# Hybrid backbone block: S5 and recurrent inputs of segment 2 are projected ahead of values, keys and queries

## The chip, the cores and the metric

The kernel runs on one core of one Trainium2 chip. The metric is the device time of one execution in microseconds (us), from the first to the last instruction of the program. Engines are named TensorE (PE in the profile; PEld is its weight load), VectorE (DVE), ScalarE (ACT), GpSimd (POOL) and SyncE (SP), which here only issues DMAs.

## The reference

One layer of a backbone block over 2048 latent tokens and 256 context tokens, 1024 features. Cut to what matters here:

```python
z = modulated_rmsnorm(x) @ w_in          # one combined input projection
q, k, v, gate, lr, lx, lgate, u = split(z)
gla = gated_linear_attention(q, k, v, lr)     # two directions, chunks, states
lru = rglru(short_conv(lx))                   # two directions, linear scan
s5  = s5(u)                                   # two directions, scanned in column-major grid order
cat = concat(norm(gla) * silu(gate), lru * gelu(lgate), glu(gelu(s5 + D * u)))
x   = x + gate1 * (cat @ w_out)
x   = x + gate2 * (square(relu(modulated_rmsnorm(x) @ w1)) @ w2)
out = rmsnorm(x)
```

The latent scans start from the final states of the context, in both directions. The S5 scan goes over the grid by columns, so each of its runs needs the input u of all four segments of latent tokens.

## The kernel before

Tokens are worked in segments: the context (`c`, 256) and four latent segments 0 to 3 of 512. All products of the projections are done in three matmuls on exact high and low parts (`mm3`, L324 to L326: `wH*hH`, `wH*hL`, `wL*hH`). A projection tile is 128 output features of one segment: eight steps over the features, 24 matmuls of 512 columns, into an `acc` tile of PSUM; ScalarE copies it out (`evac`, L331) and GpSimd's queue writes it to DRAM scratch (`put`). Its weights are loaded by the SP queue and split by `wsplit` (L318 load, L319 ScalarE cast, L320 VectorE difference) into a few rotating buffers. The values (`v_cols`) go the other way round, 272 columns at a time, and end in small transposes (L387, L390).

The tiles of a segment have three groups: `A4` (`su0 su1`, the S5 input; `lx0 lx1`, the input of the recurrent unit), `B6` (values, keys, queries) and `G4` (the gates). `in_proj` walks a list of (names, segments) that is written out by hand; `("h", s)` normalizes and splits the input of a segment (`h_of`, `hprep`, L287 to L307), for which two pairs of buffers rotate.

Beside this main stream run side streams, each a Python generator that yields the time that its step is reckoned to take, or the name of an event that has to be emitted first. `Streams.run` lets the side stream that is furthest behind take a step whenever its reckoned time, its yields times a ratio, has fallen behind the main stream's. A projection tile counts 5.2 units, a block of values 2.8. The side streams:

- `xstream` (ratio 3.0): S5 matrices (`s5_prep`) and tables (`s5_tables`), then 16 S5 runs (`s5_run`), each 1.8 units times 3.0. A run waits for its half of the S5 input in all segments (`su0` or `su1`). It loads about 1 MB, multiplies (L783), turns and scans on VectorE (L790 to L815), multiplies again (L820 to L824) and stores its result (L829).
- `ystream`, `ystream2` (ratio 0.8): the GLA's first part (`gla_prep`, L873 to L953) by pairs of blocks: segment 2 first, then 3, in each of the two streams. A segment's part waits for its `v0 v1 k0 k1 q0 q1`. Four working buffers (`wg`) hold one pair, so a stream's segment 3 follows when segment 2 has given them up. `gla_ends` (L965) comes last and gives the event `gla`.
- the recurrent unit (`lru`, ratio 4.0): forward over the context, 0, 1, backward over 3, then forward over 2 and 3; it waits for `lx0`, `lx1`.
- `read_out(3)` (ratio 0.7): it waits for `gla` and for the gates of segment 3. Blocks 3 and 2, then 1 and 0: loads (L1064 to L1067), scores (L1078, L1079), masks (L1081 to L1083), the backward state (L1028), products (L1091, L1092), a norm (L1099 to L1110) and the split of the result (L1015, L1016). The same four `wg` buffers hold one pair of blocks. Then the gate of the recurrent unit and, after the event `s5`, that of the S5 group (L1146).

`out_proj(3)` follows `in_proj` in the main stream: first products with six of the eight input parts, then the first phase's memory is given up (`open_ff`), then the rest, and the second norm. The second phase is the MLP of segments 3, 2, 1, 0, with the read-out of the next segment as a side stream.

The order in which instructions are emitted sets their priority; a scheduler then writes each engine's own queue, in which an instruction that is ready by its reckoning can come ahead of an earlier one that is not. Some parts (`wsplit`, `put`, `hprep`) are given a higher priority. On the chip each engine runs its queue in order.

Of the kernel before, what the change touches and what calls it, by code (L numbers as in the profile page):

```python
# [8 lines left out]
F32 = mybir.dt.float32  # L9
# [7 lines left out]
P = 128  # L17
# [6 lines left out]
NS = 16          # S5 groups  # L24
T8 = 8           # tokens that share a column of the S5 input layout
T16 = 16         # S5 chunk
NCH = SEQ // T16  # latent chunks
CCH = CTX // T16  # context chunks
NP = T16 + 2     # powers of the transition
XSZ = 1312  # L30
PKW = 1408       # S5 matrices of a group: read-out 2 x 256, input 4 x 128, kernel 3 x 128
# [11 lines left out]
# columns of the packed per-feature vector table  # L43
# [9 lines left out]
# W_in column tiles of 128 features  # L53
COLS = ["su0", "su1", "lx0", "lx1", "k0", "k1", "q0", "q1", "gg0", "gg1", "gg2", "gg3", "lg0", "lg1"]
WIDX = {n: i for i, n in enumerate(COLS)}
VN = 272         # half of v and the decay ranks of one direction


class Streams:
    """Emits a main and several side streams of instructions in step.  # L60

    A stream yields the time that its step takes, or the name of an event that has to be emitted first."""
# [10 lines left out]
    def step(self, limit):  # L73
        """One step of the side stream that is furthest behind; False if none is ready before `limit`."""
        ready = [x for x in self.live if (x[3] is None or x[3] in self.done) and (limit is None or x[2] <= limit)]
        if not ready:
            return False
        x = min(ready, key=lambda y: y[2])
        x[3] = None
        try:  # L80
            r = next(x[0])
        except StopIteration:
            self.live.remove(x)
            return True
        if isinstance(r, str):
            x[3] = r
        else:
            x[2] += r * x[1]
        return True

    def run(self, main):
        """`main` with the side streams."""
        while True:
            r = next(main, None)
            if r is None:
                return
            if isinstance(r, str):
                while r not in self.done:
                    assert self.step(None), (r, [x[3] for x in self.live])
                continue  # L100
            self.tm += r
            while self.step(self.tm):
                pass
            for x in self.live:
                if x[3] is not None and x[3] not in self.done:
                    x[2] = max(x[2], self.tm)
# [12 lines left out]
def hybrid_block(ctx: ExitStack, tc: tile.TileContext, xT, ctxT, cc, cct, wmodA, wmodT, pv, win, wva, wvb, upw, lrini, lruw, s5v, gluw,  # L119
# [27 lines left out]
    # ---------------------------------------------------------------- constants  # L147
# [14 lines left out]
    gsc1 = consts.tile([P, 16], F32, name="gsc1")      # norm1*(1+sc1): latent, context  # L162
    gsc2 = consts.tile([P, 8], F32, name="gsc2")

    # DRAM scratch, one tile per token segment
# [22 lines left out]
    qq_d = dram.tile([8, P, 1024], F32, name="qq_d")      # by pairs of blocks  # L188
    kk_d = dram.tile([8, P, 1024], F32, name="kk_d")
    ds_d = dram.tile([NB, 64, 512], F32, name="ds_d")      # backward block updates  # L190
    sf_d = dram.tile([16, 64, 512], F32, name="sf_d")      # forward states that enter the blocks
    bs_d = dram.tile([64, 512], F32, name="bs_d")          # backward state carried to the next segment
    # constant rows and borders of the scratch
# [7 lines left out]
    # ---------------------------------------------------------------- pools of the first phase  # L201
# [4 lines left out]
    def slots(tag, size, bufs):  # L206
        """A rotating workspace of `bufs` slots of `size` floats a partition."""
        def w(*shape, rows=P, dtype=F32):
            n = 1
            for d_ in shape:  # L210
                n *= d_
            t = side.tile([P, size], dtype, name=tag, tag=tag, bufs=bufs)[0:rows, 0:n]
            if len(shape) == 2:
                t = t.rearrange("p (a b) -> p a b", b=shape[1])
            elif len(shape) == 3:
                t = t.rearrange("p (a b c) -> p a b c", b=shape[1], c=shape[2])
            elif len(shape) == 4:
                t = t.rearrange("p (a b c d) -> p a b c d", b=shape[1], c=shape[2], d=shape[3])
            return t
        return w  # L220
# [6 lines left out]
    def big_pair():  # L227
        """The two parts of a split operand of 512 tokens."""
# [4 lines left out]
    # ---------------------------------------------------------------- adaLN vectors  # L233
# [3 lines left out]
    # silu(c) on every partition, for the products that run along the free axis  # L237
# [8 lines left out]
    def mod_first():  # L246
        """shift and scale of the first norm, latent and context"""
# [35 lines left out]
    # ---------------------------------------------------------------- normalized, modulated, split input  # L283
    def hprep(pool, src, t0, n, hH, hL, gsc, sh):
        """Normalize and modulate n tokens of src and split them exactly into two fp32r parts."""
        x = pool.tile([P, KT, n], F32, name="x", tag="x", bufs=XB)
        S.dma_start(x, src[:, t0:t0 + n].rearrange("(k p) t -> p k t", p=P))  # L287
        # 1/rms over the features on every partition
# [20 lines left out]
    def wsplit(pool, src, shape, tag, bufs, parts=None):  # L309
        """Load a weight tile and split it exactly into two fp32r parts (in `parts`, if they are there already);  # L310
        bufs: of the load, of each part."""
# [16 lines left out]
    # ---------------------------------------------------------------- input projection  # L328
# [40 lines left out]
    def v_cols(c, chunks):  # L369
        """Half of the values, token by token, with the decay ranks of one direction."""  # L370
# [50 lines left out]
    # ---------------------------------------------------------------- RG-LRU  # L421
# [21 lines left out]
    def lru(d, order, wl=wl):  # L443
        for s in order:
# [31 lines left out]
            # gates; sigmoid(z) = (1 + tanh(z/2))/2  # L476
# [35 lines left out]
    # ---------------------------------------------------------------- S5  # L512
# [4 lines left out]
    def s5_params():  # L517
# [73 lines left out]
        def cmul(or_, oi, ar, ai, br, bi, t, conj_b=False, neg_i=False):  # L591
            """(or, oi) = a*b (conj(b) if conj_b); oi negated if neg_i."""
# [51 lines left out]
        # step[k] = e^{+-i theta T 2^k}: + on the forward half, - on the backward half  # L644
# [7 lines left out]
        # input matrix  # L652
# [20 lines left out]
        # powers by slot: E: forward j, backward 17-j;  F: forward 15-s, backward s  # L673
# [13 lines left out]
    def s5_prep(b):  # L687
# [5 lines left out]
        # C lambda^k by slot  # L693
# [22 lines left out]
        # intra-chunk kernel, both directions  # L716
# [11 lines left out]
        # shifted windows of it make the Toeplitz blocks  # L728
# [9 lines left out]
    def s5_tables(g0):  # L738
        """Phase tables of four groups by doubling."""
# [23 lines left out]
    def s5_run(g):  # L763
# [32 lines left out]
        # real scans; results shifted by one chunk so that a chunk's column holds the state that enters it  # L796
# [9 lines left out]
        # the state that enters latent chunk c sits at column c + CCH + 1 on both halves  # L806
# [25 lines left out]
    # ---------------------------------------------------------------- GLA, first part: decays and block states  # L832
# [18 lines left out]
    def gla_prep(s, blocks, other=False):  # L851
        """Decays, decayed queries and keys, block updates, forward states of pairs of blocks of a segment.

        other: in the memory that the input's norm has left."""
# [15 lines left out]
        for b in blocks:  # L870
# [19 lines left out]
            # -log_sigmoid(z) = max(-z, 0) + log(1 + exp(-|z|))  # L890
# [49 lines left out]
            # forward states  # L940
# [16 lines left out]
    def gla_ends():  # L957
        """-log_sigmoid of the (shifted) token past the end of each sequence"""
# [15 lines left out]
    # ================================================================ read-out and MLP  # L974
# [15 lines left out]
    def ws(s, n, tag="t"):  # L990
        """Workspaces of the read-out, n tiles of 512; the last segment's come before the MLP's memory is there."""
# [11 lines left out]
    def decays():  # L1003
        # exponents of the decay between a block's anchor and the state that enters it
        # forward: -c_mid/16; backward: -(c_127 - c_mid + c_0 of the next block)/16
# [14 lines left out]
    def back_step(ss, blk):  # L1020
        """backward state that enters latent block blk -> ss[64:128]"""
# [17 lines left out]
    def open_ff():  # L1039
        """The first phase's workspaces make room for the MLP's."""  # L1040
# [8 lines left out]
    def read_out(s):  # L1049
        """Read-out of the three groups of a segment."""  # L1050
# [6 lines left out]
        # GLA read-out, pairs of blocks from the last to the first as the backward state runs  # L1057
# [55 lines left out]
        # RG-LRU gate  # L1113
# [14 lines left out]
        # S5 gate  # L1128
# [24 lines left out]
    def out_proj(s):  # L1153
        """Output projection, residual and second norm of a segment."""
        early = []
        if s == 3:
            # the first products run while the S5 group's read-out comes to its end
# [33 lines left out]
        # second norm; its split result takes the place of the split read-out  # L1191
# [102 lines left out]
    # ================================================================ first phase  # L1294
# [23 lines left out]
    def ystream2():  # L1318
        for x in (2, 3):
# [13 lines left out]
                          (B6, [0, 1]), (G4, [0]), ("h", 3), (G4, [1]), ("h", 2), (A4, [3]), (B6, [3, 2]), (A4, [2]),  # L1333
# [3 lines left out]
    # ================================================================ second phase  # L1337
# [8 lines left out]
def pack(i):  # L1346
    """Lay the inputs out for the kernel; no arithmetic."""
# [38 lines left out]
    # decay projection: rank rows of the two directions and, on row 16, the bias  # L1386
# [27 lines left out]
    # constants of the shapes: identity, 1+identity, strict upper mask, block starts  # L1414
# [3 lines left out]
    low = np.tri(P, P, -1, dtype=f4)     # [j, i]: 1 where j > i  # L1418
# [25 lines left out]
```

## Time and profile before

| what | value |
|---|---|
| timed runs | 2481.51, 2481.51, 2481.74 us; median 2481.51 |
| profiled execution | span 2482.1 us; no other time is given for it |
| TensorE busy | 2347.2 us (95%), 10992 matmul records |
| VectorE busy | 1610.0 us (65%) |
| ScalarE busy | 1169.2 us (47%) |
| DMA | 364.03 MB, mean 147 GB/s |

The span is the metric as the profiled execution has it. Busy time of TensorE counts matmuls that overlap as one stretch. All times in rows of the trace are in us from the start of the span.

### The profile page before, as it was taken

How to read it: one execution, taken by the hardware profiler on the slowest of the kernel's cores; microseconds unless marked ns; L12 is line 12 of the kernel's file. 1: busy time of each engine (PE TensorE's matmuls, PEld its weight loads, DVE VectorE, ACT ScalarE, POOL GpSimd, SP SyncE). 2: the span in 40 equal slices, each digit the busy share in tenths (PEclk: the TensorE clock that was granted, in tenths of full speed). 3: DMA queues.
4: the chain of work that ended last, by engine and by line, in shares of the span. 5: the costliest groups of instructions: out<-in, count | busy, mean ns of one | idle time of the engine just before them, and what ended most of it. 6: DMA issues, size and time to landing. Idle time of an engine off the chain costs nothing.

```text
span 2482.1 us, 29891 instructions
## 1 busy us (share of the span) xinstructions
PE 2347.2 (95%) x10992; PEld 1886.0 (76%) x10992; DVE 1610.0 (65%) x2698; ACT 1169.2 (47%) x1704; POOL 100.7 (4%) x141
## 2 busy tenths in 40 slices
PE   7779999898887899999999999999999999999997
PEld 3668777877675677888877788887778888888886
DVE  6886878726786766565576656557655655655555
ACT  3764567436555645343355534336543433433333
POOL 1020111002100000000000000000000000000000
PEclk9989999999998999999999999999999999999999
DMA  7666777557775643322355322336522232333221
GB/s 258 209 201 208 223 238 227 168 174 207 253 240 181 206 135 120 101 94 93 100 177 162 118 86 93 102 102 202 159 85 94 94 102 87 126 102 102 94 94 51
DMA packets 189107, 364.03 MB, mean 147 GB/s; under 512 B 35200, under 2 KB 104144, under 8 KB 187920
## 3 DMA queue, kind: packets, MB, share of 16 engines
q1 hardware_dynamic: 183872, 346.20, 44.1%
q0 software_dynamic: 5088, 15.93, 1.9%
q8 instruction: 86, 1.41, 0.2%
q14 instruction: 61, 0.50, 0.1%
HBM read 299.76 MB, written 62.75 MB: 146 GB/s over the span
## 4 chain that ended last, share of the span: by engine, by line
PE 64%; ACT 5%; DVE 5%; DMA 3%; issue 2%; SPq 1%; POOL 0%; DVEq 0%; ACTq 0%; POOLq 0%
PE acc L324 10%; PE acc L326 9%; PE acc L325 9%; PE sa L324 9%; PE sa L325 9%; PE sa L326 9%; PE sb L324 2%; PE sb L326 2%; PE sb L325 2%; DVE wL L320 1%; ACT wH L319 1%; PE sb L1146 1%; DMA t<-lru 1%; DMA t<-kk_d 0%; DMA wR<-in_wout_dram 0%
## 5 line engine op out<-in xcount | busy, mean ns | idle before, releaser
L319 ACT CAST wH<-wR 128x1024 fp32r<-128x1024 f32 (+1 forms) x353 | 370.9, 1051 | 903.9 <-PE sa L325 432.8
L324 PE MATMUL acc<-hH,wH 128*128 128x512 f32 (+1 forms) x1576 | 629.6, 400 | 24.8 <-ACT hH L303 9.2
L320 DVE TENSOR_TENSOR wL<-wR,wH 128x1024 fp32r<-128x1024 f32 (+1 forms) x353 | 427.3, 1222 | 346.5 <-ACT wH L319 342.0
L326 PE MATMUL acc<-hH,wL 128*128 128x512 f32 (+1 forms) x1576 | 620.1, 394 | 3.2 <-DVE wL L320 3.1
L325 PE MATMUL acc<-hL,wH 128*128 128x512 f32 (+1 forms) x1576 | 617.7, 392 | 1.2 <-DVE hL L307 0.8
L1257 DVE SCALAR_TENSOR_TENSOR xa<-sa,modl,xa 128x512 f32<-128x512 f32 (+1 forms) x520 | 383.1, 741 | 197.5 <-PE sa L326 194.8
L324 PE MATMUL sa<-sH,wH 128*128 128x512 f32 (+1 forms) x1040 | 403.9, 389 | 4.6 <-DVE xa L1257 4.2
L326 PE MATMUL sa<-sH,wL 128*128 128x512 f32 (+1 forms) x1040 | 402.2, 387 | 0.0
L325 PE MATMUL sa<-sL,wH 128*128 128x512 f32 (+1 forms) x1040 | 401.9, 386 | 0.0
L324 PEld LDWEIGHTS acc<-hH,wH 128*128 128x128 f32 x1576 | 299.8, 191 | 95.3 <-ACT hH L303 10.3
L325 PEld LDWEIGHTS acc<-hL,wH 128*128 128x128 f32 x1576 | 300.1, 191 | 70.8 <-issue 6.2
L326 PEld LDWEIGHTS acc<-hH,wL 128*128 128x128 f32 x1576 | 299.5, 190 | 70.8 <-DVE wL L320 5.2
L324 PEld LDWEIGHTS sa<-sH,wH 128*128 128x128 f32 x1040 | 195.2, 188 | 49.2 <-DVE xa L1257 9.3
L326 PEld LDWEIGHTS sa<-sH,wL 128*128 128x128 f32 x1040 | 195.3, 188 | 40.8
L325 PEld LDWEIGHTS sa<-sL,wH 128*128 128x128 f32 x1040 | 195.4, 188 | 40.6 <-DVE sL L1233 0.8
L1233 DVE TENSOR_TENSOR sL<-sr,sH 128x512 fp32r<-128x512 f32 x128 | 88.2, 690 | 27.6 <-ACT sH L1232 27.5
L325 PE MATMUL acc<-wL,hH 128*128 128x272 f32 x288 | 87.8, 305 | 8.8 <-DVE wL L320 8.7
L324 PE MATMUL acc<-wH,hH 128*128 128x272 f32 x288 | 89.2, 310 | 2.0 <-ACT ev L331 1.9
L331 ACT COPY ev<-acc 128x512 f32<-128x512 f32 (+2 forms) x96 | 47.5, 495 | 85.1 <-issue 41.0
L326 PE MATMUL acc<-wH,hL 128*128 128x272 f32 x288 | 86.5, 301 | 0.0
L1232 ACT CAST sH<-sr 128x512 fp32r<-128x512 f32 x128 | 78.8, 617 | 10.8 <-PE sa L326 9.0
L1231 ACT ACTIVATE sr<-sr 128x512 f32<-128x512 f32 x128 | 80.8, 632 | 3.4
(402 smaller groups left out, 2717.2 us busy)
## 6 DMA issues: line engine op xcount, KB each, us to landing
wR<-in_w_dram SPq DMA_DIRECT2D x256, 512.0 KB
wR<-in_win_dram SPq DMA_DIRECT2D x54, 512.0 KB
wm<-in_wmodT_dram SPq DMA_DIRECT2D x32, 512.0 KB
wR<-in_wout_dram SPq DMA_DIRECT2D x32, 512.0 KB
wm<-in_wmodA_dram SPq DMA_DIRECT2D x8, 1024.0 KB
x<-in_xT_dram SPq DMA_DIRECT2D x8, 1024.0 KB
w<-pk_d SPq DMA_DIRECT2D x16, 512.0 KB
xa<-in_xT_dram SPq DMA_DIRECT2D x32, 256.0 KB
```

Of the source, the lines that this page charges most:

```text
L319: A.copy(Hf, raw)
L320: V.tensor_tensor(Lf, raw, f32(Hf), OP.subtract)
L324: T.matmul(acc, wH, hH, start=first, stop=False)
L325: T.matmul(acc, wH, hL, start=False, stop=False)
L326: T.matmul(acc, wL, hH, start=False, stop=last)
L331: A.copy(e, acc)
L1146: T.matmul(ps, gw[:, k, ct * P:(ct + 1) * P], sg[k], start=k == 0, stop=k == 1)
L1231: A.activation(r, r, AF.Square)
L1232: A.copy(sH, r)
L1233: V.tensor_tensor(sL, r, f32(sH), OP.subtract)
L1257: V.scalar_tensor_tensor(xa[:, m, a0:a1], acc, modl[:, 40 + m:41 + m], xa[:, m, a0:a1], OP.mult, OP.add)
```

## The change

In the list that `in_proj` walks, the entry of `A4` for segment 2 moves from behind `B6` of segments 3 and 2 to ahead of it. All else in the diff is comments, docstrings and blank lines.

```diff
     A4, G4, B6 = "su0 su1 lx0 lx1", "gg0 gg1 gg2 gg3 lg0 lg1", "v0 v1 k0 k1 q0 q1"
     st.run(chain(in_proj([("h", "c"), ("h", 0), (A4 + " v0 v1 k0 k1", ["c"]), ("h", 1), (A4, [0]), (A4, [1]),
-                          (B6, [0, 1]), (G4, [0]), ("h", 3), (G4, [1]), ("h", 2), (A4, [3]), (B6, [3, 2]), (A4, [2]),
+                          (B6, [0, 1]), (G4, [0]), ("h", 3), (G4, [1]), ("h", 2), (A4, [3]), (A4, [2]), (B6, [3, 2]),
                           (G4, [3]), (G4, [2])]),
                  out_proj(3)))
```

## Rows read from the trace of the kernel before

**Rows 1.** First line of the page.

```profile
span 2482.1 us, 29891 instructions
```

**Rows 2.** Stretches: length; busy us (records) of PE, PEld, DVE, ACT, POOL; clock; DMA.

```profile
422.00:500.00 78.00, 70.54 (x493) 63.95 (x492) 57.82 (x132) 38.17 (x66) 5.82 (x8) 0.93 0.56 166
500.00:545.00 45.00, 43.21 (x191) 35.33 (x189) 13.19 (x29) 8.45 (x14) 3.79 (x7) 1.00 0.60 181
545.00:666.00 121.00, 107.08 (x528) 86.41 (x527) 77.40 (x136) 72.51 (x112) 22.80 (x32) 0.96 0.71 216
666.00:771.00 105.00, 85.80 (x515) 70.87 (x514) 90.91 (x212) 69.13 (x126) 5.13 (x9) 0.94 0.73 225
...
851.00:2482.00 1631.00, 1607.49 (x7206) 1305.05 (x7205) 995.79 (x1311) 689.19 (x937) 3.71 (x6) 1.00 0.35 112
```

**Rows 3.** The same stretches, records of L783 (first matmuls of S5 runs) alone.

```profile
545.00:666.00 121.00, 7.96 (x40) 6.87 (x40) 0.96 0.71 216
666.00:771.00 105.00, 16.51 (x88) 15.27 (x88) 0.94 0.73 225
```

**Rows 4.** The same stretches, records of L324 (first of each mm3) alone.

```profile
545.00:666.00 121.00, 38.05 (x93) 17.91 (x93) 0.96 0.71 216
666.00:771.00 105.00, 14.14 (x35) 6.58 (x35) 0.94 0.73 225
```

**Rows 5.** Timeline of TensorE around an S5 run: start, length, line.

```profile
701.47 0.49 PE L823 MATMUL sa<-w 128*128 128x128 f32 x2
...
702.91 1.29 PE L783 MATMUL sa<-w 128*128 128x160 f32 x8
...
704.49 0.38 PE L1092 MATMUL mm<-wg,fs 128*128 128x128 f32 x2
```

**Rows 6.** Timeline of TensorE: GLA's first matmuls, S5's, GLA's last, read-out's first.

```profile
545.17 1.13 PE L895 MATMUL sb<-glt,upt 48*128 48x256 f32 x4
...
569.89 0.90 PE L783 MATMUL sa<-w 128*128 128x160 f32 x2 [5.41 <-ACT w L777]
...
657.77 1.05 PE L965 MATMUL sb<-wg,upt 48*128 48x2 f32 x8
...
676.72 0.37 PE L1078 MATMUL sb<-wg 64*128 64x128 f32 x1 [0.34 <-DMA wg<-kk_d]
```

**Rows 7.** Timeline of the SP queue: first load of each pair of blocks.

```profile
666.00 0.37 SPq L1064 DMA_DIRECT2D wg<-gg  x1
...
716.25 0.38 SPq L1064 DMA_DIRECT2D wg<-gg  x1
```

**Rows 8.** Timeline of VectorE: last split of the GLA read-out.

```profile
772.16 0.68 DVE L1016 TENSOR_TENSOR hL<-wg,hH 128x512 fp32r<-128x512 f32 x1
```

**Rows 9.** Groups by line, 666 to 771: count, busy us, mean ns, idle before.

```profile
L1101 ACT ACT_TABLE_LOAD x4 | 5.1, 1283 | 0.1
...
L480 PE MATMUL sb<-wl,lwt 128*128 128x512 f32 x10 | 5.1, 613 | 0.3 <-DVE wg L1081 0.3
...
L1028 DVE SCALAR_TENSOR_TENSOR fs<-fs,bdec 64x128 f32<-64x128 f32 x12 | 3.8, 349 | 2.2 <-DMA fs<-ds_d 2.0
...
L1082 DVE COPY_PREDICATED wg<-mup,sb 128x512 f32<-128x512 int32 x4 | 2.9, 722 | 0.0
```

**Rows 10.** Waits of TensorE, 545 to 771: total us, times, longest.

```profile
PE sa L823 <- DVE w L814: 18.2, 12, 5.2
...
PE sb L928 <- issue: 5.3, 1, 5.3
```

**Rows 11.** Timeline of TensorE: first matmul of the values of segment 3.

```profile
422.14 0.28 PE L324 MATMUL acc<-wH,hH 128*128 128x272 f32 x1
```

**Rows 12.** Timeline of VectorE: last low parts of segment 2's input.

```profile
421.78 1.67 DVE L307 SCALAR_TENSOR_TENSOR hL<-x,modl,hH 128x256 fp32r<-128x256 f32 x4
```

**Rows 13.** Waits of ScalarE, 545 to 771: total us, times, longest.

```profile
ACT wH L319 <- PE acc L325: 30.7, 10, 7.9
```

**Rows 14.** Ten us around the wait of L928, columns as in rows 2.

```profile
620.00:630.00 10.00, 4.71 (x17) 3.84 (x16) 7.12 (x8) 6.80 (x12) 5.10 (x6) 0.72 0.66 230
```

## The prediction

> **What bounds the kernel now.** I read the page first for the span [rows 1], then cut the span into stretches at the places where the work changes [rows 2], then counted what runs in each, then asked who waits. From 851 us to the end TensorE is busy 1607.49 of 1631 us: the MLP is bound by TensorE and nothing before it changes what it has to do, so the question is when it can begin. Before that, three stretches differ. From 500 to 545 us (keys and queries of segments 3 and 2) TensorE is busy 43.21 of 45 us and VectorE 13.19: TensorE-bound, VectorE empty. From 545 to 666 TensorE is busy 107 of 121 us. From 666 to 771 it is TensorE 85.80 and VectorE 90.91 of 105 us.
>
> What fills the last two is seen by counting. An S5 run has 8 records of L783 and a projection tile of 512 tokens 8 of L324. So 545 to 666 holds 40/8 = 5 S5 runs and 93/8 = 11.6 projection tiles; 666 to 771 holds 11 runs and 4.4 tiles [rows 3, 4]. The 16 tiles are those of segment 2's first group (4) and of the two gate groups (12). By adding the planner's yields only 4.5 of them come before the end of the GLA part; the trace has 11.6 there, so projections are pulled ahead wherever a chain makes TensorE wait, and the last 105 us are left with little filler. There the S5 runs follow each other every 105/11 = 9.5 us, since TensorE's queue has a run's first matmuls (L783) behind the last ones (L823, L824) of the run before [rows 5], and between a run's first and last VectorE has to turn and scan.
>
> The second chain is the GLA. Its first decay matmul (L895) starts at 545.17 us, the moment that q1 of segment 2 is done; its end (L965) comes at 657.77, the read-out's loads start at 666.00, its first scores at 676.72, its second pair of blocks is loaded from 716.25, and the last split of its result (L1016) starts at 772.16 [rows 6 to 8]. So from q1_2 to the first output products are 121 + 105 = 226 us. Both chains end together, around 775 us.
>
> **The change part by part.** No instruction is added or removed: four tiles (su0, su1, lx0, lx1 of segment 2) move from behind the values, keys and queries to ahead of them. The planner's sums then shift: su0_2 is done 86.4 units earlier (248.2 for 334.6), so S5 runs begin at 300.2 (the tables are ready then) and not at 334.6; the RG-LRU of segments 2 and 3 comes at 286 to 361, not 350 to 413; and q1_2, with it the whole GLA of segments 2 and 3, leaves the planner 20.8 units later (350.2 for 329.4). At 350.2 S5 runs 0 to 8 have been emitted; before, none had at 329.4. I take the new stretches in turn.
>
> *Up to q1_2, now 422 to 545.* TensorE gets more to do ahead of q1_2: four tiles of 24 matmuls at 43.21/191 = 0.226 us, the pace of 500 to 545 [rows 2], are 21.7 us; nine S5 runs at 3.02 us, the unbroken run from 701.47 to 704.49, are 27.2; two RG-LRU gate sets of 8 records at 0.51 us (5.1/10) [rows 9] are 8.2. The waits of L823, 18.2 us over 12 [rows 10], are 1.5 each on a loaded VectorE; on a free one I take 0.4, 3.6 for nine. Sum 61 us. From below: 422 to 500 holds 78 - 70.54 = 7.5 us without TensorE [rows 2], into which S5 matmuls can go: 54. From above 66: those waits doubled, and the 1.4 us of the next sentences. I take 61, since those 7.5 us are waits of TensorE's own in-order queue. The moved tiles need segment 2's normalized input at once: the values start at 422.14 and the last four parts of hL are written from 421.78 for 1.67 us [rows 11, 12]. The tiles take their k-th part only after k times 0.7 us, so nothing, at most 1.4 us; the cover is thin, and if it goes the whole queue shifts by as much.
>
> *GLA, now 545 to 666.* It finds the same company: five runs (9 to 13) and 11.6 of the 12 gate tiles, pulled ahead as before. What goes is the wait of run 0 for its own projection, 5.41 us at 569.89 [rows 6], and the slow clock behind it, 1.6 us. The other wait, L928 for 5.3 us [rows 10], stays, being GLA's own chain. So 121 - 7 = 114 us. From below: ScalarE waits 30.7 us in this and the next stretch for TensorE to release a weight buffer [rows 13], ten waits, with GLA's activations behind them in its queue; without two of the longest, 2 x 7 us, it would be 100. From above 121. I take 114.
>
> *Read-out of segment 3, now 666 to 771.* Here the S5 runs are gone but two (14 and 15), and so are both RG-LRU gate sets. A pair of blocks alone: loads 676.72 - 666.00 = 10.7 us [rows 6, 7]; three mask operations for each block at 0.72, 4.3; eight steps of the backward state at 0.35, 2.8; two table loads at 1.28 and four activations at about 0.7, 5.4; eight gains as long as those steps, 0.35, and two products of 0.7, 4.2 [rows 9]; about 68 TensorE records at 0.11 us (28 records in the 3.02 us of [rows 5]), 7; copies, squares, casts and differences not covered, 2.6. Sum 37 us, some 4 of which the two blocks overlap: 33. Two pairs, the second loaded only when the first gives up its buffers: 66 us. From above the 105 of now; between ends so far apart it lies near the first, because most of what shared VectorE's 90.91 us has left; two runs' worth on top, 68 us. As 0.4 tiles are left to fill TensorE, it stands idle here, and after waits it drops to the lower of its two levels: 0.72 granted from 620 to 630 [rows 14]. Its 7 us a pair doubled are 14 more, so 82 is the upper end; 58 the lower, if the pairs overlap more.
>
> The Trainium skill (TensorE: Matmul & The Clock Gate, section on HAM oscillation) says that idle stretches bring the throttled level back each time; the trace agrees at 620 to 630, and the rule speaks against this change. By it alone the sum would be 14 us more.
>
> *Behind it.* From 771 to 851 the output products, the reopening of the pools and the second norm follow as now, without run 15's last part: 1.5 us less, 0 to 2. The MLP's 1631 us stay.
>
> Sum: +61 - 7 - 37 - 1.5 = +15.5 us. The profiled execution took 2482.1 us, 0.6 us above the median of the runs (2481.51); so 2482.1 + 15.5 - 0.6 = **2497 us**, slower. What replaces the S5 chain as the last to end is the read-out behind a GLA that starts 61 us later.
>
> **The rivals.** *Faster: the S5 chain was the bound and its cover is free.* For it: 16 S5 runs pace the time from 569.89 to 771, VectorE is 87% busy at the end and 29% busy at 500 to 545, where nine runs move to. It decides if GLA and read-out together need less than 226 - 61 = 165 us. At the lower ends, 54 - 21 (100 for GLA) - 47 (58 for the read-out) - 2 is -16: 2466 us. Against it: 114 + 68 = 182. The Trainium skill (Perfetto Trace Analysis, Optimization Strategy) advises to interleave regimes with different most-contended engines, which is this; the trace has the two regimes, but the rule does not say what is put off. By it the time would be that of this rival.
>
> *No change: the two shifts cancel.* The queues don't follow the planner strictly (11.6 tiles for 4.5), so GLA at 104 us and the read-out at 62 would give +61 - 17 - 43 - 1.5, within a microsecond of zero: 2481 us. For it: both chains end together now. Against it: a coincidence of two sizes.
>
> *Much slower: the read-out also meets the lower clock.* The upper ends of the first and third term: +66 - 7 - 23 = +36 us: 2518. For it: the missing filler. Against it: most of the read-out is on ScalarE, VectorE and the queues.
>
> **How the numbers follow.** Forecast 0.50, faster 0.26, no change 0.13, much slower 0.11. The forecast's own range, from the mixed bounds of its terms, is 2487 to 2512. A measurement of this kernel tells some 0.2%, 5 us, from no change: faster 0.26, same 0.13, slower 0.61. The range reaches to the faster rival's 2466 and to 2520, just past the last one; each side leaves about 0.1.
>
> **What would show it.** Right: L783 first appears some 50 us ahead of 569.89 while keys and queries run; L895 of segments 2 and 3 starts near 606 us instead of 545; S5 is done before the read-out's second pair; TensorE has holes between about 725 and 790 us with waits of L1078, L1091 or the output products on loads, VectorE or ScalarE; the last L1016 of the GLA part is near 788; the stretch behind it is as long as now. Wrong in the terms: L895 before 595 (S5 found holes), GLA under 105 us (its waits were TensorE's pace, not its own), a read-out under 60 us. Wrong altogether: no hole in TensorE up to the output products.

## The result, and the profile after

The change makes the kernel slower: 2499.0 us median of four runs (2494.3 to 2501.3) against 2481.6 (2481.5 to 2481.9), a ratio of 1.0069 with a 95% interval of 1.0056 to 1.0082. The forecast was 2497. The profiled execution after has a span of 2499.5 us, 17.4 us more than [rows 1].

Stretches of the kernel after, cut where the work changes, with the columns of [rows 2]:

```profile
545.00:611.00 66.00, 60.75 (x323) 49.16 (x322) 40.04 (x96) 25.19 (x55) 3.24 (x6) 1.00 0.62 188
611.00:725.00 114.00, 97.09 (x485) 79.03 (x485) 77.30 (x135) 64.83 (x100) 18.03 (x32) 0.94 0.71 213
725.00:787.00 62.00, 40.58 (x246) 33.14 (x244) 37.16 (x90) 36.95 (x58) 1.62 (x3) 0.85 0.59 170
867.00:2499.00 1632.00, 1607.39 (x7207) 1305.30 (x7206) 995.71 (x1311) 688.20 (x937) 3.69 (x6) 1.00 0.34 112
```

The second and third answer to the GLA part and the read-out of [rows 2]. The read-out is short now, but TensorE is busy in only 40.58 of its 62 us, and its granted clock has dropped to 0.85. The MLP is the same to a tenth of a microsecond of TensorE work.

The same for L783 alone, the first matmuls of S5 runs (eight records each), as in [rows 3]:

```profile
500.00:545.00 45.00, 4.26 (x24) 3.47 (x24) 1.00 0.68 201
545.00:611.00 66.00, 7.93 (x48) 7.12 (x48) 1.00 0.62 188
611.00:726.00 115.00, 7.65 (x40) 6.42 (x40) 0.94 0.71 211
726.00:787.00 61.00, 2.59 (x16) 2.31 (x16) 0.84 0.60 172
```

Nine runs stand ahead of the GLA, five beside it, two beside the read-out, as forecast. Timelines of TensorE, the SP queue and VectorE, three engines in order; they answer to [rows 6 to 8]:

```profile
610.95 1.99 PE L895 MATMUL sb<-glt,upt 48*128 48x256 f32 x8
...
642.06 0.90 PE L783 MATMUL sa<-w 128*128 128x160 f32 x2 [7.37 <-ACT w L777]
...
725.67 1.05 PE L965 MATMUL sb<-wg,upt 48*128 48x2 f32 x8
...
787.27 0.80 PE L324 MATMUL acc<-hH,wH 128*128 128x512 f32 x1 [7.84 <-ACT hH L1015]
...
725.23 0.45 SPq L1064 DMA_DIRECT2D wg<-gg  x1
...
787.25 0.69 DVE L1016 TENSOR_TENSOR hL<-wg,hH 128x512 fp32r<-128x512 f32 x1 [0.74 <-ACT hH L1015]
```

So the GLA starts 65.8 us later than before, its ends 67.9 later, the read-out's loads 59.2 later, and the last split of the GLA's result 15.1 later. Behind that nothing is regained. Some waits of TensorE from 600 to 870 us (total, times, longest):

```profile
PE acc L324 <- ACT hH L1015: 9.2, 2, 7.8
...
PE acc L324 <- ACT hH L1201: 6.3, 1, 6.3
PE sa L823 <- DVE w L814: 6.1, 4, 4.0
...
PE sb L1078 <- DMA wg<-kk_d: 4.2, 1, 4.2
...
PE mm L1091 <- issue: 2.5, 1, 2.5
PE sb L1099 <- ACT wg L1094: 2.4, 2, 1.2
```

These are the forecast's holes: TensorE now waits for the read-out itself (the 6.3 us before L1201, in the second norm, are there before the change too). The 7.8 us are the first output products waiting for the split of the last pair. From 422 us to the MLP, TensorE is busy 372.0 of 429 us before and 376.2 of 445 after: no work was added (1976 and 1980 records), but there are 11.8 us more of idle time, and the same matmuls are busy 4.2 us longer.

### The profile page after: what moved, and what is told of

Same layout as the page of the kernel before. It is cut to its first block, busy times and chain, and to the rows that moved or that the text cites. A ratio compares the mean times of both kernels' runs of the same rounds, so it can differ in the third digit from the quotient of the medians.

```text
span 2499.5 us, 29912 instructions
## 1 busy us (share of the span) xinstructions
PE 2348.0 (94%) x10992; PEld 1882.8 (75%) x10992; DVE 1614.5 (65%) x2698; ACT 1168.7 (47%) x1704; POOL 95.9 (4%) x141
## 4 chain that ended last, share of the span: by engine, by line
PE 68%; DVE 7%; ACT 6%; DMA 4%; issue 3%; SPq 1%; POOL 0%; DVEq 0%; ACTq 0%; POOLq 0%
PE acc L324 11%; PE acc L326 10%; PE acc L325 10%; PE sa L324 9%; PE sa L325 9%; PE sa L326 9%; PE sb L324 2%; PE sb L326 2%; PE sb L325 2%; DVE wL L320 1%; ACT wH L319 1%; DMA w<-pk_d 1%; PE mm L1091 1%; PE mm L1092 1%; PE sb L1146 1%
## 5 line engine op out<-in xcount | busy, mean ns | idle before, releaser
L324 PE MATMUL acc<-hH,wH 128*128 128x512 f32 (+1 forms) x1576 | 633.0, 402 | 32.8 <-ACT hH L303 9.7
L324 PE MATMUL sa<-sH,wH 128*128 128x512 f32 (+1 forms) x1040 | 403.9, 389 | 5.7 <-DVE xa L1257 5.3
L324 PEld LDWEIGHTS acc<-hH,wH 128*128 128x128 f32 x1576 | 300.7, 191 | 104.3 <-ACT hH L1015 10.8
L324 PEld LDWEIGHTS sa<-sH,wH 128*128 128x128 f32 x1040 | 195.2, 188 | 50.1 <-DVE xa L1257 10.2
L324 PE MATMUL acc<-wH,hH 128*128 128x272 f32 x288 | 87.4, 304 | 1.9 <-ACT ev L331 1.9
```

The source lines that it names most:

```text
L324: T.matmul(acc, wH, hH, start=first, stop=False)
```

## The experiments

The theory at the start: what TensorE does ahead of q1 of segment 2 sets the start of the GLA, and the GLA with the read-out then ends last. The rivals: the S5 runs were the bound; or TensorE's total work sets the end, wherever it stands. Runs on different chips scatter more than the four above (kernel before: 2473 to 2488), so every time is compared with runs of the kernel before on the same chip. The first five columns are starts in the profiled execution, in us: the GLA's first matmul (L895), its last ones (L965), the last split of its result (L1016), the last store of an S5 run (L829), and the S5 gate's matmuls (L1146, behind which the output products go on). Line numbers are those of the kernel before.

| kernel | L895 | L965 | GLA's split | S5's store | L1146 | median us | ratio to before, 95% |
|---|---|---|---|---|---|---|---|
| before | 545.2 | 657.8 | 772.2 | 779.4 | 787.0 | 2481.6 | |
| after | 610.9 | 725.7 | 787.3 | 765.0 | 802.1 | 2499.0 | 1.0069 (1.0056 to 1.0082) |
| hold_both | 565.5 | 666.0 | 763.9 | 793.5 | 800.6 | 2501.9 | 1.0079 (1.0061 to 1.0096) |
| su_only | 587.4 | 699.0 | 785.0 | 753.1 | 800.1 | 2496.2 | 1.0051 (1.0034 to 1.0068) |
| lx_only | 562.1 | 679.2 | 763.8 | 799.0 | 805.8 | 2500.0 | 1.0073 (1.0057 to 1.0089) |
| b6_first | 511.9 | 608.7 | 762.0 | 769.4 | 788.7 | 2487.6 | 1.0023 (1.0011 to 1.0034) |
| half_s5_after | 610.2 | 701.2 | 761.7 | 600.7 | 777.2 | 2466.0 | 0.9946 (0.9927 to 0.9965) |
| half_s5_before | 546.3 | 658.7 | 754.8 | 705.8 | 769.3 | 2458.9 | 0.9918 (0.9903 to 0.9933) |
| hold_gates | 605.7 | 715.2 | 781.8 | 753.7 | 797.4 | 2499.1 | 1.0084 (1.0056 to 1.0112) |
| lx_late | 526.4 | 636.7 | 765.5 | 756.8 | 792.9 | 2482.3 | 1.0020 (1.0009 to 1.0031) |
| hold_s5_tail | 606.2 | 697.6 | 788.4 | 789.6 | 802.9 | 2502.5 | 1.0087 (1.0071 to 1.0102) |
| lx_late_lru | 521.5 | 631.8 | 774.0 | 767.3 | 789.1 | 2488.4 | 1.0020 (1.0008 to 1.0032) |
| cut_tiles | 551.4 | 663.8 | 787.5 | 794.8 | 802.4 | 2488.5 | 1.0026 (1.0014 to 1.0038) |
| q2_first | 537.3 | 645.0 | 769.5 | 777.4 | 785.0 | 2481.5 | 0.9998 (0.9990 to 1.0007) |

The table shows which chain ends last. In most kernels L1146 comes 14.5 to 15.6 us behind the GLA's last split. In hold_both and lx_only it comes 7 us behind S5's last store instead, and in b6_first and lx_late 4 to 5 us behind the recurrent unit's last split (784.4 and 788.0). In the kernel before, cut_tiles and q2_first the GLA and S5 end together: both gaps are there, 15 us and 7.6 or 7.7.

**Only the tiles ahead (hold_both).** To the kernel after:

```diff
+        yield "q1_2"
         for g in range(NS):
             yield from s5_run(g)
...
-    st.add(chain(lru(1, ["c"]), lru(0, ["c", 0, 1]), lru(1, [3]), lru(0, [2, 3])), RZ)
+    st.add(chain(lru(1, ["c"]), lru(0, ["c", 0, 1]), lru(1, [3]), after_q(), lru(0, [2, 3])), RZ)   # after_q: yield "q1_2"
```

> The changed order, but no S5 run and no RG-LRU gate set of segments 2 and 3 is emitted before q1 of segment 2, so that only the four moved tiles come ahead of it. My theory (TensorE's work ahead of q1 sets the start of the GLA, and 22 of the 66 us are the tiles, the rest S5 runs and gates): L895 of segments 2 and 3 starts at 567 to 572 us, S5 begins about where it began before the change (570), read-out and S5 end together again at 773 to 787, time 2482 to 2495. Rival (the S5 runs and gates went into holes of TensorE, the tiles and something else made the delay): L895 still starts near 606 to 611 and the time stays at 2495 to 2500.

TensorE's L895, first start 565.5 us (count; min/median/max ns; first and last start):

```profile
L895 PE MATMUL sb<-glt,upt x32: 376/376/480, 565.5 to 622.4; 48*128 48x256 f32 x32
```

The start is 1.5 us below the theory's range, and the rival on it falls: 20.3 of the 65.8 us are the four tiles (with one S5 run's first matmuls). The time is a miss: with the tiles alone ahead, the kernel is as slow as with the whole change. Yet another chain ends last here. The GLA, which starts 20 us later than before, has its last split 8 us earlier; S5, whose first run starts 6 us earlier than before, has its last store 14 us later, and L1146 comes 7 us behind it. The last store before the change, then in hold_both the GLA's last split and the last store:

```profile
779.43 0.59 SPq L829 DMA_DIRECT2D y<-w  x1
```

```profile
763.94 0.68 DVE L1016 TENSOR_TENSOR hL<-wg,hH 128x512 fp32r<-128x512 f32 x1
...
793.51 0.60 SPq L829 DMA_DIRECT2D y<-w  x1
```

So in hold_both S5 sets the end and not the GLA. The GLA part is 100 us long, and from its end to L1146 it takes 134.6 us (before: 129.2). Two stretches, with the columns of [rows 2]:

```profile
565.50:666.00 100.50, 91.92 (x457) 74.59 (x456) 75.40 (x127) 68.90 (x105) 22.11 (x32) 0.95 0.77 232
666.00:801.00 135.00, 99.10 (x553) 84.07 (x553) 95.50 (x233) 66.11 (x128) 2.21 (x5) 0.85 0.65 192
```

Behind the GLA TensorE idles 36 of 135 us at a clock of 0.85. Eleven S5 runs stand there (twelve before), with fewer tiles between them, and their last result matmuls (L823) start at 792.1 and not at 778.4. TensorE's largest sum of waits from 565 to 801 us is for loads of S5 runs; L783 has no such wait in the kernel before:

```profile
PE sa L783 <- DMA w<-pk_d: 12.4, 3, 5.5
```

Why these loads came late was not tested.

**Two tiles at a time (su_only, lx_only).** The plan of `in_proj`, first su_only, then lx_only:

```diff
-("h", 2), (A4, [3]), (A4, [2]), (B6, [3, 2]),
+("h", 2), (A4, [3]), ("su0 su1", [2]), (B6, [3, 2]), ("lx0 lx1", [2]),
+("h", 2), (A4, [3]), ("lx0 lx1", [2]), (B6, [3, 2]), ("su0 su1", [2]),
```

> Only su0 and su1 of segment 2 move ahead; lx0 and lx1 stay behind. My theory: two tiles (11 us) and some seven S5 runs (25 us with their waits) come ahead of q1, the two gate sets do not; L895 starts at 580 to 592; the gates come back into the GLA part or the read-out; time 2480 to 2492, between the two kernels. Rival (the S5 chain was the bound, and the gates and lx tiles ahead of q1 hid its gain): S5 ends early, time under 2475.

> Only lx0 and lx1 of segment 2 move ahead; su0 and su1 stay behind, so that no S5 run can come ahead of q1. My theory: two tiles and two gate sets, L895 at 562 to 568 (17 to 23 us later than before); the S5 runs start that much later too, both chains end later by about as much, less the gates that have left the read-out: 2488 to 2502. Rival (the read-out was bound by the gates beside it): under 2480.

The starts of the GLA are as expected in both. The time of su_only is 4 us above its range: seven S5 runs ahead of q1 did not pay for two tiles. That also speaks against the S5 chain as the bound there, which would have made it the fastest. In lx_only one gate set came ahead, not two. S5 begins at 586.8, 16.9 us later than before, and its last store is 19.6 us later, while the GLA's last split comes 8 us earlier: not both chains are late, as expected, but S5 alone, and it sets the end.

**The other direction (b6_first, lx_late, lx_late_lru, q2_first).** Tiles are put further back than in the kernel before:

```diff
-("h", 2), (A4, [3]), (B6, [3, 2]), (A4, [2]),
+("h", 2), (B6, [3, 2]), (A4, [3]), (A4, [2]),                                   # b6_first
+("h", 2), ("su0 su1", [3]), (B6, [3, 2]), ("su0 su1", [2]), ("lx0 lx1", [3]), ("lx0 lx1", [2]),   # lx_late
+("h", 2), (A4, [3]), (B6, [2, 3]), (A4, [2]),                                   # q2_first
```

lx_late_lru is lx_late with the recurrent unit of segments 3 and 2 on a stream of its own:

```diff
-    st.add(chain(lru(1, ["c"]), lru(0, ["c", 0, 1]), lru(1, [3]), lru(0, [2, 3])), RZ)
+    st.add(chain(lru(1, ["c"]), lru(0, ["c", 0, 1])), RZ)
+    st.add(lru_late(), 1.5)        # waits for lru1_c and lru0_1, then lru(1, [3]), lru(0, [2, 3])
```

> The order before the change, but values, keys and queries of segments 3 and 2 come ahead of segment 3's first group as well; the S5 input is complete at the same place as before. My theory (the GLA with the read-out and the S5 chain end together before the change): L895 starts near 523, the first S5 run stays near 570, the read-out's loads begin near 645, and the S5 runs still go on to about 771: 2472 to 2482. Rival (GLA and read-out alone set the end): the whole 22 us come out, 2460. Rival (the S5 chain alone set the end): no change, 2481.

> The kernel before with the four lx tiles of segments 3 and 2 put behind everything that S5 and the GLA wait for (su of 3; values, keys and queries of 3 and 2; su of 2; then lx). Both the GLA and the S5 chain can begin two tiles, 11 us, earlier: L895 near 534, first L783 near 559; the four tiles are then filler behind. By my theory (what counts is how long the two chains run behind q1 and whether TensorE has filler there): 2472 to 2480, faster. Rival (the end is TensorE's total work, which is the same): 2480 to 2484. Rival (the RG-LRU, now last, delays the output products): over 2486.

> The order with the lx tiles last, and besides it the RG-LRU of segments 3 and 2 on a stream of its own with a third of its delay (ratio 1.5 instead of 4), so that its gates are emitted as soon as the lx tiles are there. In the run before it the RG-LRU was the last of the three chains: S5 ended its last run at 761, the GLA's read-out at 766, the RG-LRU's split only at 788. My theory (the chain that ends last alone sets the end): the output products of the S5 gate start at 775 to 783 instead of 793, time 2466 to 2476, faster than before the change. Rival (VectorE is shared, and the other two chains lose what the RG-LRU gains): 2479 to 2486.

> The order before the change, but values, keys and queries go over segment 2 first and segment 3 second in each pair, so that q1 of segment 2 is done half a tile pair, 5.4 us, earlier and nothing else moves. If the start of the GLA alone set the end, 2476 or 2477. By my theory (S5 and read-out end together, the S5 chain starts where it did): 2478 to 2484, no change that can be measured.

No gain in any of them, and all but q2_first are above the theory's range. In b6_first the GLA starts 33 us earlier (22 expected), but S5's first run at 610.9 us, 41 later and not near 570, and S5 then runs to 767; the recurrent unit's split comes last (784.39). Its time is above every range that was given. In lx_late the GLA is 19 and S5 19.5 us earlier; there too the recurrent unit's split is last (787.98), while the time lies in the range of the rival on total work. With that unit's gates done 58 us sooner (lx_late_lru: last L480 at 707.7 for 766.0), its split comes only 6 us sooner, at 781.95, and the GLA's last split 8 us later, at 773.98 for 765.50, with the other gates now beside it: with one chain pulled ahead another became later, as the rival has it. The time, 2488.4 us, is 2 us above the rival's range too, and that VectorE is what they share was not tested. q2_first starts the GLA 8 us earlier and S5 where it was, and changes nothing. The three chains of the kernel before end within 8 us of each other (772.2, 779.4 and 780.0), and pulling one or two ahead leaves the rest.

**Half of S5 left out (half_s5_after, half_s5_before).** For groups 8 to 15 the S5 input is copied to the output and nothing is computed:

```diff
+        if g >= NRUN:                      # 8
+            ur0 = w(256)
+            S.dma_start(ur0, su_l[:, ch].rearrange("s h r w -> s h (r w)"))
+            S.dma_start(y_d[g // 8][:, (g % 8) * 16:(g % 8 + 1) * 16, :, :], ur0.rearrange("p (r w) -> p r w", r=4))
+            yield 0.5
+            return
```

> The changed kernel without the computation of S5 runs 8 to 15 (their input is copied to the output instead): some 24 us of TensorE work and as many VectorE scans less. If the GLA with the read-out is the chain that sets the end after the change, as I hold, only run 8 goes from ahead of q1 (3 us) and two runs from beside the read-out (3 to 6 us): L895 near 607, time 2488 to 2496. Rival (TensorE's total work sets the end, whatever the order): all 24 us of the work come out, 2470 to 2478.

> The kernel before without the computation of S5 runs 8 to 15. There all eight lay beside the read-out (666 to 771). If the S5 runs are what stretched that read-out to 105 us, it falls to 65 to 80 us and the time to 2442 to 2460. Rival (the read-out is as long by its own chain and loads): less than 8 us come out, above 2473.

The first is a miss. L895 stays at 610.2, but the GLA part shrinks from 114.7 us to 91.0 and the time falls by some 31 us (0.9946 against 1.0069, times 2482; 24.9 of it by L1146), far past the theory's range and past the rival's. L965 in half_s5_after (line 972 there):

```profile
L972 PE MATMUL sb<-wg,upt x8: 247/248/268, 701.2 to 702.0; 48*128 48x2 f32 x8
```

So the GLA part is not as long as its own chain: the five S5 runs beside it cost 23.7 us, 4.7 each. And the end moves with the GLA: its end comes 24.5 us earlier, L1146 24.9. In half_s5_before four runs stay beside the GLA, which keeps 112 us, and the eight that are missing behind it save 18.6 us from there to L1146, 2.3 each; the time, at the upper end of what was expected, falls by 20 us. The read-out itself takes 87.8 us from its first load (666.97) to its last split, more than the 65 to 80 expected, with four S5 runs still beside it.

**S5 runs moved from the GLA to the read-out (hold_s5_tail).** To the kernel after:

```diff
+        if g >= 9:
+            V.tensor_copy(ur[:, 0:1], c0s[:, 0, NB:NB + 1])   # written by gla_ends; the load overwrites it
         S.dma_start(ur[:, 0:32], su_c[:, ch, :])
...
         for g in range(NS):
+            if g == 9:
+                yield "gla"
             yield from s5_run(g)
```

> The changed kernel with S5 runs 9 to 15 held back by a data dependence (one column of their input buffer is first written from the GLA's last decays) until the GLA part is done. My revised theory, after the run that left half of S5 out: the GLA part of 115 us is not as long as its own chain, the five S5 runs beside it cost it some 4.8 us each, while beside the read-out a run costs 2.2. So the GLA part falls to 91 to 97 us, the read-out grows by about 11 and the time falls to 2482 to 2492. Rival (the GLA was as long as its chain and the gain of that run came from elsewhere, or the tiles take the freed places): the GLA part stays above 108, the seven runs are only later, and the time is 2505 to 2525.

The GLA part is 91.4 us, as the revised theory says, in a kernel that leaves nothing out. But the gain is gone by L1146: 105.3 us behind L965 for 76.4, 5.8 for each of the five runs and not 2.2, and the time is 10 us above the theory's range. TensorE's waits for VectorE from 500 to 870 us (line 825 is L823 of the kernel after, where they are 11.9 us over 12):

```profile
PE sa L825 <- DVE w L816: 22.1, 11, 8.5
```

**Tiles held back as filler (hold_gates).** The kernel after with the last three gate tiles of segment 2 loaded only when the GLA's ends are written:

```diff
-(G4, [3]), (G4, [2])]
+(G4, [3]), ("gg0 gg1 gg2", [2]), ("wait", "gla"), ("gg3 lg0 lg1", [2])]   # "wait": yield "gla"
...
+        if after is not None:                    # in wsplit, c0s[:, 0, NB:NB + 1] for these three tiles
+            V.tensor_copy(raw[:, 0:1], after)
         S.dma_start(raw, src)
```

> The changed kernel with the last three gate tiles of segment 2 (28 us of TensorE) held back by a data dependence until the GLA's ends are done, so that they are there to fill the read-out. If the GLA part (115 us) is as long as its own chain, it stays within 8 us of that, the holes only change places, and the time stays at 2493 to 2504. Rival (the pulled-ahead tiles slow the GLA): the GLA part falls by 15 us or more and the time to 2478 to 2488.

The times are as the theory expects: GLA part 109.5 us, then 82.2 (76.4 in the kernel after), the whole unchanged. But the test is weaker than it was meant to be. Three tiles are 72 matmuls, 16 us at the pace of [rows 2] and not 28; and half of that stood behind the GLA already, so the records of L324 beside the GLA fall only from 84 to 72, at a granted clock of 0.89 for 0.94.

**Filler taken away (cut_tiles).** The kernel before, with gg2, gg3, lg0 and lg1 of segment 2 cut to the first of their eight parts:

```diff
+                    kt = 1 if s == 2 and name in ("gg2", "gg3", "lg0", "lg1") else KT
                     for k in range(KT):
-                        mm3(acc, wH[:, k, :], wL[:, k, :], hH[:, k, :], hL[:, k, :], k == 0, k == KT - 1)
+                        if k < kt:
+                            mm3(acc, wH[:, k, :], wL[:, k, :], hH[:, k, :], hL[:, k, :], k == 0, k == kt - 1)
```

> The kernel before with four of the gate tiles of segment 2 (gg2, gg3, lg0, lg1) cut to the first of their eight parts of the product, 4 x 21 matmuls or 19 us of TensorE work less, all of it behind q1. If tiles behind q1 are filler in the waits of the three chains, as my theory has it after the run with only the four tiles moved, little comes out: 2473 to 2482. Rival (TensorE's work sets the end wherever it stands): the whole 19 us, 2460 to 2466.

Beyond the theory's range, and away from the rival: with 84 matmuls less the kernel is not faster but 0.3% slower. The stretch behind the GLA, first in the kernel before, then in cut_tiles:

```profile
658.00:787.00 129.00, 108.06 (x622) 87.90 (x622) 106.13 (x253) 81.93 (x152) 5.13 (x9) 0.95 0.73 224
```

```profile
658.00:787.00 129.00, 96.29 (x502) 82.26 (x501) 103.27 (x245) 75.90 (x143) 4.81 (x10) 0.80 0.67 208
```

120 records fewer (84 cut, the rest later), yet only 11.8 us less busy time: the clock falls from 0.95 to 0.80. The result matmuls of the S5 runs, each on its run's chain, become slower (count; min/median/max ns; first and last start); before, then cut_tiles:

```profile
L823 PE MATMUL sa<-w x64: 270/275/579, 584.2 to 778.4; 128*128 128x128 f32 x64
```

```profile
L825 PE MATMUL sa<-w x64: 270/415/582, 590.5 to 793.8; 128*128 128x128 f32 x64
```

This profiled execution was the slowest of its kernel's six, 10 us above the median, so its starts are not compared to the microsecond. Counted from its own L965, the stretch to L1146 is 138.6 us for 129.2. The mean granted clock is low in all six, 0.971 to 0.975, where the 17 runs of the kernel before on that chip have 0.978 to 0.984. The rule that TensorE's total work sets the end falls with this run: taking these tiles from behind q1 gained nothing. That the lower clock alone ate the gain was not tested apart.

## Why the prediction was right

**Up to q1_2: forecast +61 (54 to 66), measured +65.8.** Right, at the upper end. hold_both gives the tiles 20.3 (forecast 21.7), so the rest cost 45.4: the two gate sets are 16 records of L480, busy 7.5 us (8.2), and eight further S5 runs 37.9, or 4.7 each (3.02 and 0.4 of wait); su_only gives 4.6, with seven runs and two tiles. That price per run is the term that was mis-sized: an unbroken run of matmuls doesn't show what waits around it. The input of segment 2 cost nothing; the moved tiles start without a wait.

**GLA: forecast 121 - 7 = 114, measured 114.3 from L895 to the read-out's first load.** The size is right and the reason wrong. The 7 us that were to go did not: in place of run 0's wait of 5.41 us at 569.89 another run waits 7.37 at 642.06, for ScalarE's copy of its input (L777), and no row gives the 1.6 us of slow clock. From L895 to L965 the part even grew, from 112.6 to 114.7. What went lies behind L965: the first load came 8.2 us after it and now comes 0.4 us ahead of it. The SP queue before, and after:

```profile
660.11 0.50 SPq L774 DMA_DIRECT2D w<-tb_d  x1
665.14 0.63 SPq L829 DMA_DIRECT2D y<-w  x1
666.00 0.37 SPq L1064 DMA_DIRECT2D wg<-gg  x1
```

```profile
723.85 0.64 SPq L770 DMA_DIRECT2D w<-su_c  x1
724.58 0.48 SPq L1025 DMA_DIRECT2D fs<-ds_d  x1
725.23 0.45 SPq L1064 DMA_DIRECT2D wg<-gg  x1
```

Before, the read-out's first load stood behind an S5 run's store (L829), for which the in-order queue stood still from 660.6 to 665.1. The store waited for ScalarE's copies (L827) of the run's result. In ScalarE's queue those stood behind the gates of the recurrent unit (L481, L486), but the result itself was ready late, with the last of the run's matmuls (L824). ScalarE, then TensorE:

```profile
661.53 1.28 ACT L481 ACT_TABLE_LOAD   x1
662.83 1.27 ACT L481 ACTIVATE wl<-sb,hb 128x512 f32<-128x512 f32 x2
663.99 0.81 ACT L486 ACTIVATE wl<-wl,nsp 128x512 f32<-128x512 f32 x1
664.69 0.43 ACT L827 COPY w<-sa 128x128 f32<-128x128 f32 x2
```

```profile
663.79 0.39 PE L824 MATMUL sa<-w 128*128 128x128 f32 x2
```

The result was there by 664.18 (663.79 and 0.39), so the gates can have put the copies off by at most 0.5 us; the rest of the store's wait was for the S5 run. After, no store that waits is in the way. The stop of 4.5 us is half of the 8.7 that went; the other half was not traced. The lower bound of 100, taken from ScalarE's waits, was for the wrong cause: what the part can lose is its five S5 runs (91 us without them).

**Read-out: forecast 105 to 68 (58 to 82), measured 106.2 to 62.0,** from the first load to the last split. Right in kind; the forecast was 6 us too long; the two S5 runs beside it cost nothing that shows (L965 to L1146 is 76.4 us with them, 76.0 in half_s5_after without). That this chain sets the end holds: L1146 is 14.8 us behind its last split, 14.9 before, while S5's last store is 37 us ahead of L1146. The lower clock came, as the rule of the Trainium skill (TensorE: Matmul & The Clock Gate, section on HAM oscillation) said of idle stretches: 0.85 granted for 0.94 in [rows 2]; but the read-out came out 6 us shorter than its sum, so the 14 us more were not added.

**Behind: forecast -1.5, measured +0.7** from the last split to the second norm's L1193 (834.6 before, 850.3 after), and +1.7 from there to the end. Sum: 65.8 - 6.5 - 44.2 + 0.7 + 1.7 = 17.5 us, the 17.4 of the spans. The first term came out 5 us too small and the read-out's 7 us too large (-44.2 for -37): errors of opposite sign make the total better than its terms, and that is luck.

**The rivals.** The S5 chain as the bound with free cover falls: su_only and the whole change have S5 done 47 and 37 us ahead of L1146 and are slow. Interleaving the regimes (the Trainium skill, Perfetto Trace Analysis, Optimization Strategy) was done by the change: the S5 runs beside the keys and queries cost 45 us with the gates ahead of the GLA, and against hold_both, where they stand behind, the time is the same. With it the kernel is 0.7% slower than before, so the advice brought no gain here.

**What the forecast did not have.** It put the loss down to all that goes ahead of q1. hold_both, with the tiles alone ahead, is as slow as the kernel after (1.0079 and 1.0069, with intervals that overlap), but the two have not one cause: after the change the GLA with the read-out ends last, in hold_both S5 does. So what share of the 17.4 us the tiles have, and what the S5 runs and gates, is not shown. What makes an S5 run cost 4.7 to 5.8 us in three places and 2.3 behind the GLA of the kernel before, TensorE's queue, VectorE or the SP queue, was not told apart; nor was the clock's part in hold_both separated from the missing tiles' and the late loads'.

## What to carry to other kernels

Ask of independent work not only how long it takes but where it stands. Ahead of the start of a chain it puts that start off by its whole time (20.3 us for four tiles); whether the end moves as much depends on which chain is then last, and two orders can be equally slow for different reasons. So read in every run which chain the end follows, before the times are compared. A sum over stretches has to price each piece of work by the place it moves to. When several chains end together, an order that helps one shows no gain, and leaving out one piece of work at a time shows which are paid for.

## What the runs showed of the hardware

Taking matmuls out of a stretch with waits need not shorten it: with 19 us of work less the granted clock was 0.80 and not 0.95 over 129 us of the profiled execution, the S5 result matmuls' median was 415 ns and not 275, and the kernel was 0.3% slower. And an in-order queue passes a wait on: a store on the SP queue stood 4.5 us, at least 4 of them for its S5 run to end, and the first load of another chain stood behind it.
